# RMSNorm with Silu on one core: 64 KB runs in three buffers and a single SyncE queue, in place of 32 KB runs in six buffers and two queues

## The chip, the cores and the metric

One core of one Trainium2 chip; the other cores idle. The metric is the device time of one execution in microseconds (us). Where two kernels are compared, both ran in the same rounds on the same chip. A quoted ratio is the mean time of one kernel's fast runs over the mean of the other's fast runs of the same rounds, so it isn't quite the ratio of the medians quoted beside it.

In the views, DVE is VectorE, ACT ScalarE, PE TensorE (PEld its weight loads), POOL GpSimd, SP or SPq SyncE, and L88 line 88 of the kernel. A line of a group ends with its count, its busy us and mean ns, and the us that its engine sat idle before it, with what ended the idle time. A line of windows has the stretch in us and its length, then the busy us of PE, PEld, DVE, ACT and POOL.

## The reference

`x` is 8 x 1024 x 2048 fp32, so 8192 rows of 2048, 67.1 MB in and 67.1 MB out.

```python
def reference(x, gamma, eps):
    rms = np.sqrt(np.mean(x ** 2, axis=-1, keepdims=True) + eps)
    out = gamma * x / rms
    return (out * (1 / (1 + np.exp(-out)))).astype(np.float32)
```

## The kernel before

A block is 512 rows, four on each of 128 partitions, 4 MB. ScalarE issues the loads, SyncE the stores: two queues. Six blocks are in flight.

```python
    J = 4
    BUFS = 6
    xb = x2.rearrange("(b p j) d -> b p (j d)", p=P, j=J)      # runs of 4 x 2048 x 4 B = 32 KB
    ...
    def load(b):
        xt = pool.tile([P, J * d], f32, name="xt")
        nc.scalar.dma_start(out=xt, in_=xb[b])                 # queue of ScalarE
    ...
    def multiply(b):                                           # x * rstd * gamma
        for j in range(J):
            nc.vector.scalar_tensor_tensor(out=row(b, j), in0=row(b, j), scalar=rstds[b][:, j:j + 1],
                                           in1=g, op0=ALU.mult, op1=ALU.mult)
    def silu(b):
        for h in range(0, J, 2):                               # two rows at a time
            cols = slice(h * d, (h + 2) * d)
            nc.scalar.activation(out=blocks[b][:, cols], in_=blocks[b][:, cols], func=ACT.Silu)
        store(b)
    def store(b):
        nc.sync.dma_start(out=ob[b], in_=blocks[b])            # queue of SyncE
    ...
```

The squares of a block's rows are shared by ScalarE (Square with an accumulator) and VectorE (a multiply-reduce); the root is ScalarE's, the reciprocal VectorE's. The last block is treated as the change treats all of them: gamma alone on VectorE, rstd as Silu's scale.

Of the kernel before, what the change touches and what calls it, by code (L numbers as in the profile page):

```python
# [1 line left out]

# [4 lines left out]

ACT = mybir.ActivationFunctionType
ALU = mybir.AluOpType


@with_exitstack
def kernel(
    ctx: ExitStack,
    tc: tile.TileContext,
    x: bass.AP,
    gamma: bass.AP,
    eps: bass.AP,
    out: bass.AP,
):  # L20





    nc = tc.nc
    P = nc.NUM_PARTITIONS
    f32 = mybir.dt.float32
    x2 = x.flatten_outer_dims()
    o2 = out.flatten_outer_dims()  # L30
    n, d = x2.shape
    J = 4
    BUFS = 6
    nblk = n // (P * J)
    xb = x2.rearrange("(b p j) d -> b p (j d)", p=P, j=J)
    ob = o2.rearrange("(b p j) d -> b p (j d)", p=P, j=J)

    singles = ctx.enter_context(tc.tile_pool(name="singles", bufs=1))
    pool = ctx.enter_context(tc.tile_pool(name="pool", bufs=BUFS))
    small = ctx.enter_context(tc.tile_pool(name="small", bufs=2))  # L40
    psum = ctx.enter_context(tc.tile_pool(name="psum", bufs=1, space=bass.MemoryType.PSUM))

    Q = 4
    w = d // Q
    grow = singles.tile([P, w], f32)
    g = singles.tile([P, d], f32)
    eps_t = singles.tile([P, 1], f32)
    ones = singles.tile([P, P], f32)
    junk_a = psum.tile([P, d], f32, name="junk_a")
    junk_v = psum.tile([P, d], f32, name="junk_v")  # L50
    blocks, sss, rmss, rstds = {}, {}, {}, {}

    def load(b):
        xt = pool.tile([P, J * d], f32, name="xt")
        nc.scalar.dma_start(out=xt, in_=xb[b])  # L55
        blocks[b] = xt

    def row(b, j):
        return blocks[b][:, j * d:(j + 1) * d]

    def squares_scalar(b, loads=()):


        sss[b] = small.tile([P, J], f32, name="ss")
        for j in range(share(b)):
            nc.scalar.activation(out=junk_a, in_=row(b, j), func=ACT.Square,  # L66
                                 accum_out=sss[b][:, j:j + 1])
            if j == 0:
                for s in loads:
                    load(s)  # L70

    def squares_vector(b):
        for j in range(share(b), J):
            nc.vector.tensor_tensor_reduce(  # L74
                out=junk_v, in0=row(b, j), in1=row(b, j), scale=1.0, scalar=0.0,
                op0=ALU.mult, op1=ALU.add, accum_out=sss[b][:, j:j + 1])

    def share(b):
        return 1 if 4 <= b <= 12 and b % 2 == 0 else 2

    def root(b):
        rms = small.tile([P, J], f32, name="rms")
        nc.scalar.activation(out=rms, in_=sss.pop(b), func=ACT.Sqrt, scale=1.0 / d, bias=eps_t)  # L83
        rmss[b] = rms

    def invert(b):
        rstd = small.tile([P, J], f32, name="rstd")
        nc.vector.reciprocal(out=rstd, in_=rmss.pop(b))  # L88
        rstds[b] = rstd

    def multiply(b):
        for j in range(J):
            nc.vector.scalar_tensor_tensor(out=row(b, j), in0=row(b, j), scalar=rstds[b][:, j:j + 1],  # L93
                                           in1=g, op0=ALU.mult, op1=ALU.mult)

    def silu(b):
        for h in range(0, J, 2):
            cols = slice(h * d, (h + 2) * d)
            nc.scalar.activation(out=blocks[b][:, cols], in_=blocks[b][:, cols], func=ACT.Silu)  # L99
        store(b)  # L100

    def store(b):
        nc.sync.dma_start(out=ob[b], in_=blocks[b])

    with tc.manual_schedule():

        for b in range(BUFS):
            load(b)
        nc.vector.memset(ones, 1.0)  # L109
        nc.vector.memset(eps_t, float(eps))  # L110
        nc.scalar.activation(out=junk_a[:, 0:1], in_=ones[:, 0:1], func=ACT.Square)  # L111
        nc.sync.dma_start(out=grow[0:P:P // Q, :],
                          in_=bass.AP(tensor=gamma.tensor, offset=gamma.offset, ap=[[w, Q], [1, w]]))
        for c in range(Q):
            k = c * (P // Q)
            nc.tensor.matmul(junk_v[:, c * w:(c + 1) * w], ones[k:k + 1, :], grow[k:k + 1, :],  # L116
                             start=True, stop=True)
        nc.vector.tensor_copy(out=g, in_=junk_v)  # L118



        last = nblk - 1
        SOON = 3
        squares_scalar(0)
        squares_vector(0)
        root(0)
        invert(0)
        for b in range(last):
            loads = [b + 3] if BUFS <= b + 3 < nblk else []
            if b < SOON:  # L130
                multiply(b)
                squares_scalar(b + 1, loads)
                silu(b)
                squares_vector(b + 1)
                root(b + 1)
            elif b < last - 1:
                squares_scalar(b + 1, loads)
                squares_vector(b + 1)
                root(b + 1)
                multiply(b)  # L140
                silu(b)
            else:
                multiply(b)
                squares_scalar(b + 1)
                silu(b)
                squares_vector(b + 1)
                root(b + 1)
            if b + 1 < last:
                invert(b + 1)


        for j in range(J):
            if j == J // 2:
                invert(last)
            nc.vector.tensor_mul(out=row(last, j), in0=row(last, j), in1=g)  # L155
        for j in range(J):
            nc.scalar.activation(out=row(last, j), in_=row(last, j), func=ACT.Silu,  # L157
                                 scale=rstds[last][:, j:j + 1])
        store(last)


# [1 line left out]
_INS = ['x', 'gamma', 'eps']  # L163
_OUTS = [((8, 1024, 2048), 'float32')]

_NUMBERS = {'eps': 9.999999747378752e-06}


# [26 lines left out]
```

## Time and profile before

| | before |
|---|---|
| time, median | 316.84 us in the first three runs, 316.9 to 317.0 in all later rounds |
| span of the profiled run | 315.1 us |
| bytes moved | 134.24 MB |
| DMA share of the two data queues | 49.7% + 49.3% |
| VectorE, ScalarE busy | 75%, 68% |

The lines behind this table are in the prediction. One kind of evidence goes below what the page prints: the trace's DMA packet records, each with queue, start, duration and size. They carry no number of the DMA engine. I assigned packets to the 16 engines by joining each packet to the one that ends where it starts (a packet typically starts 3 ns before the last one's end, so sums of gaps can be negative) and has the right size for its place in the queue; every engine then holds the same count, 256 packets before and 152 after. Tables from these records stand in plain fences.

### The profile page before, as it was taken

Reading aid. Unit: us, or ns where it says so; the run is one execution under the profiler, and the core shown is the slowest. Engines: PE = TensorE matmul, PEld = TensorE weight load, DVE = VectorE, ACT = ScalarE, POOL = GpSimd, SP = SyncE. Lnnn points to the kernel's source line nnn. Section 1 sums busy time; section 2 is a strip of 40 time slices with the busy share of each in tenths; the row PEclk is TensorE's granted clock in tenths of the full one; section 3 lists DMA queues with packets and bytes.
Section 4 is the critical chain, followed back from the end, with each engine's and each line's share of the span. In section 5 each row is a group of like instructions: output and inputs, shape, how many; then the busy total and the mean of one; then the engine's idle time right before and its main releaser. Section 6 shows DMA issues by size and latency. Waiting matters only on the chain.

```text
span 315.1 us, 436 instructions
## 1 busy us (share of the span) xinstructions
PE 2.1 (1%) x8; PEld 0.5 (0%) x8; DVE 235.3 (75%) x157; ACT 213.8 (68%) x136; POOL 0.2 (0%) x4
## 2 busy tenths in 40 slices
PE   0200000000000000000000000000000000000000
PEld 0000000000000000000000000000000000000000
DVE  0679597979995695957969489693995939999600
ACT  1349998972799258682687827877288768779910
POOL 0000000000000000000000000000000000000000
DMA  8999999999999999999999999999999999999996
GB/s 334 403 462 403 395 466 399 466 403 462 403 463 403 459 412 453 412 453 420 445 420 445 424 441 424 441 424 441 428 437 437 428 445 420 445 420 445 420 449 287
DMA packets 4618, 134.24 MB, mean 426 GB/s; under 512 B 516, under 2 KB 516, under 8 KB 520
## 3 DMA queue, kind: packets, MB, share of 16 engines
q10 hardware_dynamic: 2304, 67.11, 49.7%
q1 hardware_dynamic: 2312, 67.12, 49.3%
q14 instruction: 2, 0.02, 0.0%
HBM read 67.12 MB, written 67.11 MB: 426 GB/s over the span
## 4 chain that ended last, share of the span: by engine, by line
DMA 68%; DVE 14%; ACT 11%; issue 2%; ACTq 1%; DVEq 0%
DMA xt<-in_x_dram 68%; DVE xt L93 9%; DVE junk_v L74 5%; ACT xt L99 4%; ACT junk_a L66 3%; ACT xt L157 2%; ACT L83 1%; ACTq L190 1%; ACT L157 0%; ACT L99 0%; ACT rms L83 0%; DVE ss L74 0%; DVE rstd L88 0%; ACTq L55 0%; ACTq L83 0%
## 5 line engine op out<-in xcount | busy, mean ns | idle before, releaser
L93 DVE SCALAR_TENSOR_TENSOR xt<-xt,rstd,g 128x2048 f32<-128x2048 f32 x60 | 137.0, 2347 | 0.1
L99 ACT ACTIVATE xt<-xt 128x4096 f32<-128x4096 f32 x30 | 108.3, 3615 | 27.2 <-DVE xt L93 27.1
L74 DVE CUSTOM_DVE_ANT_0 junk_v<-xt 128x2048 f32<-128x2048 f32 x37 | 85.1, 2299 | 42.5 <-DMA xt<-in_x_dram 41.7
L66 ACT ACTIVATE junk_a<-xt 128x2048 f32<-128x2048 f32 x27 | 50.7, 1877 | 22.6 <-DMA xt<-in_x_dram 22.3
L83 ACT ACT_TABLE_LOAD x15 | 19.2, 1283 | 27.6 <-DVE ss L74 27.5
L99 ACT ACT_TABLE_LOAD x14 | 18.0, 1283 | 0.2
L118 DVE COPY g<-junk_v 128x2048 f32<-128x2048 f32 x1 | 2.3, 2292 | 9.4 <-PE junk_v L116 9.4
L88 DVE RECIPROCAL rstd<-rms 128x4 f32<-128x4 f32 x16 | 2.8, 174 | 8.3 <-ACT rms L83 8.3
L155 DVE TENSOR_TENSOR xt<-xt,g 128x2048 f32<-128x2048 f32 x4 | 8.9, 2279 | 0.0
L83 ACT ACTIVATE rms<-ss,eps_t 128x4 f32<-128x4 f32 x16 | 4.8, 297 | 5.7 <-DVE ss L74 5.5
L157 ACT ACTIVATE xt<-xt,rstd 128x2048 f32<-128x2048 f32 x4 | 7.7, 1990 | 0.0
L74 DVE DVE_READ_ACCUMULATOR2_ANT ss<- 128x1 f32 x37 | 5.2, 141 | 0.0
L66 ACT ACTIVATION_READ_ACCUMULATOR junk_a<-xt 128x1 f32 x27 | 5.0, 186 | 0.0
L111 ACT ACT_TABLE_LOAD x1 | 1.3, 1283 | 3.8 <-issue 3.8
L116 PE MATMUL junk_v<-grow,ones 1*128 1x512 f32 x8 | 2.1, 1130 | 8.2 <-DMA grow<-in_gamma_dram 8.2
L157 ACT ACT_TABLE_LOAD x1 | 1.3, 1283 | 0.0
L109 DVE MEMSET ones<- 128x128 f32 x1 | 0.2, 165 | 0.8 <-PEq L176 0.8
L116 PEld LDWEIGHTS junk_v<-grow,ones 1*128 1x128 f32 x8 | 0.5, 307 | 8.2 <-issue 8.2
L111 ACT ACTIVATE junk_a<-ones 128x1 f32<-128x1 f32 x1 | 0.2, 174 | 0.0
L176 POOL MEMSET const-bfloat16-1.0<- 128x1 bf16 x1 | 0.1, 101 | 0.0
L176 POOL MEMSET const-uint8-127<- 128x1 uint8 x1 | 0.1, 101 | 0.0
L176 POOL MEMSET const-float32-0.0<- 128x1 f32 x1 | 0.1, 98 | 0.2 <-issue 0.2
(2 smaller groups left out, 0.2 us busy)
## 6 DMA issues: line engine op xcount, KB each, us to landing
xt<-in_x_dram ACTq DMA_DIRECT2D x16, 4096.0 KB, 38.7
out_dram<-xt SPq DMA_DIRECT2D x16, 4096.0 KB, 29.0
grow<-in_gamma_dram SPq DMA_DIRECT2D x1, 8.0 KB
```

Of the source, the lines that this page charges most:

```text
L66: nc.scalar.activation(out=junk_a, in_=row(b, j), func=ACT.Square, accum_out=sss[b][:, j:j + 1])
L74: nc.vector.tensor_tensor_reduce(out=junk_v, in0=row(b, j), in1=row(b, j), scale=1.0, scalar=0.0, op0=ALU.mult, op1=ALU.add, accum_out=sss ...
L83: nc.scalar.activation(out=rms, in_=sss.pop(b), func=ACT.Sqrt, scale=1.0 / d, bias=eps_t)
L88: nc.vector.reciprocal(out=rstd, in_=rmss.pop(b))
L93: nc.vector.scalar_tensor_tensor(out=row(b, j), in0=row(b, j), scalar=rstds[b][:, j:j + 1], in1=g, op0=ALU.mult, op1=ALU.mult)
L99: nc.scalar.activation(out=blocks[b][:, cols], in_=blocks[b][:, cols], func=ACT.Silu)
L111: nc.scalar.activation(out=junk_a[:, 0:1], in_=ones[:, 0:1], func=ACT.Square)
L116: nc.tensor.matmul(junk_v[:, c * w:(c + 1) * w], ones[k:k + 1, :], grow[k:k + 1, :], start=True, stop=True)
L118: nc.vector.tensor_copy(out=g, in_=junk_v)
L155: nc.vector.tensor_mul(out=row(last, j), in0=row(last, j), in1=g)
L157: nc.scalar.activation(out=row(last, j), in_=row(last, j), func=ACT.Silu, scale=rstds[last][:, j:j + 1])
L190: with _tile.TileContext(nc) as tc:
```

## The change

The intent: longer runs (64 KB a partition), one ordered queue so that loads and stores go in blocks of 8 MB, and a multiply that doesn't wait for rstd.

```diff
-    J = 4
-    BUFS = 6
+    R = 8
+    BUFS = 3
+    loads_of[0] = [4, 4]
+    loads_of[nsup - 1] = stores_of[nsup - 1] = [4, 4]     # halves at the two ends
...
-        nc.scalar.dma_start(out=xt, in_=xb[b])
+            nc.sync.dma_start(out=xt[:, cols(lo, hi)], in_=xs[s][:, cols(lo, hi)])
...
+        for r in range(lo, mid):        # first half of the rows: ScalarE squares
+            nc.scalar.activation(out=junk_a, in_=..., func=ACT.Square, accum_out=...)
+        for r in range(mid, hi):        # second half: VectorE squares
             nc.vector.tensor_tensor_reduce(...)
...
-            nc.vector.scalar_tensor_tensor(out=row(b, j), ..., scalar=rstds[b][:, j:j + 1], in1=g, ...)
+            two = xt[:, cols(r, r + 2)].rearrange("p (r d) -> p r d", r=2)
+            nc.vector.tensor_mul(out=two, in0=two, in1=g.unsqueeze(1).to_broadcast([P, 2, d]))
...
-            nc.scalar.activation(out=blocks[b][:, cols], in_=blocks[b][:, cols], func=ACT.Silu)
+            nc.scalar.activation(out=row, in_=row, func=ACT.Silu, scale=rstd[:, r - lo:r - lo + 1])
+                    nc.sync.dma_start(out=os[s][:, cols(a, b)], in_=xt[:, cols(a, b)])
...
+        for s in range(nsup):
+            for lo, hi in pieces(loads_of[s]):
+                group(s, lo, hi)
+            if s >= 1 and s + 2 < nsup:
+                load(s + 2)
```

The order in the single queue is load 0 (two halves), 1, 2, store 0, 1, load 3, store 2, load 4, store 3, load 5, store 4, load 6, store 5, load 7 (halves), store 6, store 7 (halves): six turns from load to store and five back.

More of the change, by code (lines that the diff above doesn't have):

```diff
@@ L31 @@
     n, d = x2.shape
-    J = 4
-    BUFS = 6
-    nblk = n // (P * J)
-    xb = x2.rearrange("(b p j) d -> b p (j d)", p=P, j=J)
-    ob = o2.rearrange("(b p j) d -> b p (j d)", p=P, j=J)
+    R = 8
+    BUFS = 3
+    nsup = n // (P * R)
+    xs = x2.rearrange("(s p r) d -> s p (r d)", p=P, r=R)
+    os = o2.rearrange("(s p r) d -> s p (r d)", p=P, r=R)
+    loads_of = [[R] for _ in range(nsup)]
+    stores_of = [[R] for _ in range(nsup)]
+    loads_of[0] = [4, 4]
+    loads_of[nsup - 1] = stores_of[nsup - 1] = [4, 4]
     singles = ctx.enter_context(tc.tile_pool(name="singles", bufs=1))
@@ L44 @@
     w = d // Q
-    grow = singles.tile([P, w], f32)
     g = singles.tile([P, d], f32)
@@ L50 @@
     junk_v = psum.tile([P, d], f32, name="junk_v")
-    blocks, sss, rmss, rstds = {}, {}, {}, {}
-    def load(b):
-        xt = pool.tile([P, J * d], f32, name="xt")
-        nc.scalar.dma_start(out=xt, in_=xb[b])
-        blocks[b] = xt
-    def row(b, j):
-        return blocks[b][:, j * d:(j + 1) * d]
-    def squares_scalar(b, loads=()):
-        sss[b] = small.tile([P, J], f32, name="ss")
-        for j in range(share(b)):
-            nc.scalar.activation(out=junk_a, in_=row(b, j), func=ACT.Square,
-                                 accum_out=sss[b][:, j:j + 1])
-            if j == 0:
-                for s in loads:
-                    load(s)
@@ L72, in squares_vector @@
-    def squares_vector(b):
-        for j in range(share(b), J):
-            nc.vector.tensor_tensor_reduce(
-                out=junk_v, in0=row(b, j), in1=row(b, j), scale=1.0, scalar=0.0,
-                op0=ALU.mult, op1=ALU.add, accum_out=sss[b][:, j:j + 1])
-    def share(b):
-        return 1 if 4 <= b <= 12 and b % 2 == 0 else 2
-    def root(b):
-        rms = small.tile([P, J], f32, name="rms")
-        nc.scalar.activation(out=rms, in_=sss.pop(b), func=ACT.Sqrt, scale=1.0 / d, bias=eps_t)
-        rmss[b] = rms
@@ L86, in invert @@
-    def invert(b):
-        rstd = small.tile([P, J], f32, name="rstd")
-        nc.vector.reciprocal(out=rstd, in_=rmss.pop(b))
-        rstds[b] = rstd
-    def multiply(b):
-        for j in range(J):
-            nc.vector.scalar_tensor_tensor(out=row(b, j), in0=row(b, j), scalar=rstds[b][:, j:j + 1],
-                                           in1=g, op0=ALU.mult, op1=ALU.mult)
-    def silu(b):
-        for h in range(0, J, 2):
-            cols = slice(h * d, (h + 2) * d)
-            nc.scalar.activation(out=blocks[b][:, cols], in_=blocks[b][:, cols], func=ACT.Silu)
-        store(b)
@@ L102, in store, with cols, pieces, load @@
-    def store(b):
-        nc.sync.dma_start(out=ob[b], in_=blocks[b])
+    tiles = {}
+    def cols(lo, hi):
+        return slice(lo * d, hi * d)
+    def pieces(sizes):
+        lo = 0
+        for k in sizes:
+            yield lo, lo + k
+            lo += k
+    def load(s):
+        xt = pool.tile([P, R * d], f32, name="xt")
+        for lo, hi in pieces(loads_of[s]):
+            nc.sync.dma_start(out=xt[:, cols(lo, hi)], in_=xs[s][:, cols(lo, hi)])
+        tiles[s] = xt
+    def group(s, lo, hi):
+        xt = tiles[s]
+        k = hi - lo
+        mid = lo + k // 2
+        ss = small.tile([P, R], f32, name="ss")
+        rms = small.tile([P, R], f32, name="rms")
+        rstd = small.tile([P, R], f32, name="rstd")
+        for r in range(lo, mid):
+            nc.scalar.activation(out=junk_a, in_=xt[:, cols(r, r + 1)], func=ACT.Square,
+                                 accum_out=ss[:, r - lo:r - lo + 1])
+        for r in range(mid, hi):
+            nc.vector.tensor_tensor_reduce(
+                out=junk_v, in0=xt[:, cols(r, r + 1)], in1=xt[:, cols(r, r + 1)], scale=1.0, scalar=0.0,
+                op0=ALU.mult, op1=ALU.add, accum_out=ss[:, r - lo:r - lo + 1])
+        nc.scalar.activation(out=rms[:, 0:k], in_=ss[:, 0:k], func=ACT.Sqrt, scale=1.0 / d, bias=eps_t)
+        for r in range(lo, hi, 2):
+            if r == lo + 2:
+                nc.vector.reciprocal(out=rstd[:, 0:k], in_=rms[:, 0:k])
+            two = xt[:, cols(r, r + 2)].rearrange("p (r d) -> p r d", r=2)
+            nc.vector.tensor_mul(out=two, in0=two, in1=g.unsqueeze(1).to_broadcast([P, 2, d]))
+        for r in range(lo, hi):
+            row = xt[:, cols(r, r + 1)]
+            nc.scalar.activation(out=row, in_=row, func=ACT.Silu, scale=rstd[:, r - lo:r - lo + 1])
+            for a, b in pieces(stores_of[s]):
+                if b == r + 1:
+                    nc.sync.dma_start(out=os[s][:, cols(a, b)], in_=xt[:, cols(a, b)])
@@ L105 @@
     with tc.manual_schedule():
-        for b in range(BUFS):
-            load(b)
+        for s in range(BUFS):
+            load(s)
+        nc.scalar.dma_start(out=g[0:P:P // Q, 0:w],
+                            in_=bass.AP(tensor=gamma.tensor, offset=gamma.offset, ap=[[w, Q], [1, w]]))
         nc.vector.memset(ones, 1.0)
@@ L111 @@
         nc.scalar.activation(out=junk_a[:, 0:1], in_=ones[:, 0:1], func=ACT.Square)
-        nc.sync.dma_start(out=grow[0:P:P // Q, :],
-                          in_=bass.AP(tensor=gamma.tensor, offset=gamma.offset, ap=[[w, Q], [1, w]]))
         for c in range(Q):
             k = c * (P // Q)
-            nc.tensor.matmul(junk_v[:, c * w:(c + 1) * w], ones[k:k + 1, :], grow[k:k + 1, :],
+            nc.tensor.matmul(junk_v[:, c * w:(c + 1) * w], ones[k:k + 1, :], g[k:k + 1, 0:w],
                              start=True, stop=True)
         nc.vector.tensor_copy(out=g, in_=junk_v)
-        last = nblk - 1
-        SOON = 3
-        squares_scalar(0)
-        squares_vector(0)
-        root(0)
-        invert(0)
-        for b in range(last):
-            loads = [b + 3] if BUFS <= b + 3 < nblk else []
-            if b < SOON:
-                multiply(b)
-                squares_scalar(b + 1, loads)
-                silu(b)
-                squares_vector(b + 1)
-                root(b + 1)
-            elif b < last - 1:
-                squares_scalar(b + 1, loads)
-                squares_vector(b + 1)
-                root(b + 1)
-                multiply(b)
-                silu(b)
-            else:
-                multiply(b)
-                squares_scalar(b + 1)
-                silu(b)
-                squares_vector(b + 1)
-                root(b + 1)
-            if b + 1 < last:
-                invert(b + 1)
-        for j in range(J):
-            if j == J // 2:
-                invert(last)
-            nc.vector.tensor_mul(out=row(last, j), in0=row(last, j), in1=g)
-        for j in range(J):
-            nc.scalar.activation(out=row(last, j), in_=row(last, j), func=ACT.Silu,
-                                 scale=rstds[last][:, j:j + 1])
-        store(last)
+        for s in range(nsup):
+            for lo, hi in pieces(loads_of[s]):
+                group(s, lo, hi)
+            if s >= 1 and s + 2 < nsup:
+                load(s + 2)
 _INS = ['x', 'gamma', 'eps']
```

## The prediction

> **What bounds the kernel now.** I read the page's totals first, then its slices, then the DMA queues. The totals and the queues:
>
> ```profile
> span 315.1 us, 436 instructions
> PE 2.1 (1%) x8; PEld 0.5 (0%) x8; DVE 235.3 (75%) x157; ACT 213.8 (68%) x136; POOL 0.2 (0%) x4
> ...
> DMA packets 4618, 134.24 MB, mean 426 GB/s; under 512 B 516, under 2 KB 516, under 8 KB 520
> ...
> q10 hardware_dynamic: 2304, 67.11, 49.7%
> q1 hardware_dynamic: 2312, 67.12, 49.3%
> ```
>
> No compute engine is over 75%, while the two queues together hold the 16 DMA engines for 99% of the span (q10 is the loads, issued by ScalarE; q1 the stores, issued by SyncE). Is that 99% real work, or is the rate different when loads and stores share the engines? The windows of the trace answer it: loads alone, the start of sharing, sharing, and the end where the last stores run alone. The last two columns are DMA share and GB/s.
>
> ```profile
> 3.00:40.00 37.00, 2.09 (x8) 0.55 (x8) 24.14 (x17) 24.26 (x20) 0.00 (x0) 1.00 1.00 425
> 40.00:80.00 40.00, 0.00 (x0) 0.00 (x0) 36.42 (x26) 28.26 (x21) 0.00 (x0) 1.00 1.00 433
> 80.00:280.00 200.00, 0.00 (x0) 0.00 (x0) 158.16 (x104) 140.47 (x85) 0.00 (x0) 1.00 1.00 432
> ```
>
> The share is 1.00 in all three. The rate is 432 to 433 GB/s in the shared part and 425 in the first 37 us, where two short disturbances lie (below). The chain that ended last says the same: 68% of it is waiting for loads.
>
> ```profile
> DMA 68%; DVE 14%; ACT 11%; issue 2%; ACTq 1%; DVEq 0%
> ```
>
> Below the page I used the trace's DMA packet records. All 4096 data packets are 32,768 B; the typical one takes 1213 ns, on both queues, whether loads run alone, both alternate, or stores run alone at the end. The four packets of gamma, 2048 B each, take 84 ns. A straight line through the two sizes: (1213 - 84)/(32768 - 2048) = 0.03675 ns per byte, which is 27.2 GB/s an engine and 435 GB/s for 16, plus 84 - 75.3 = 8.7 ns per packet. One engine has 256 packets: 256 x 1.213 = 310.5 us. The first data packet starts 1.7 us into the span, the last ends at 313.9, so 312.2 us hold 310.5 us of packets. The 1.7 us that are missing: the first packet of each engine takes 1.9 us instead of 1.2 (0.7 us), around 36 to 38 us, just after the first store was issued, one packet on each engine takes 1.8 us (0.6 us), and the engines' staggered starts and ends. **The kernel is bound by DMA from end to end, and the engines are full.** The measured time is 1.7 us above the profiled span (316.84 against 315.1).
>
> **What the Trainium skill says.** (1) "DMA: Bandwidth & Descriptors", section "Where 436 GB/s comes from", gives a ceiling of 16 x 32 B x 850 MHz = 435.2 GB/s per core. The slope of my line, 435 GB/s, agrees; the sustained 432 GB/s is 99.3% of it. (2) The same page, "Why small descriptors are slow", puts a fixed cost of some cycles on each packet; the trace shows such a cost, the 8.7 ns of the line above. It is what a longer run can save, and it is small. (3) The same page, "Issuing engines are not separate DMA queues": all DMAs run on the same 16 engines whoever issues them, and several issuers save sequencer time only. The trace agrees as far as it goes: each packet takes 1213 ns with one queue at work or two. (4) "VectorE: DVE Perf Modes", "The perf-mode tier table", has an fp32 tensor_tensor at one element per cycle, 2293 ns for 2048. The trace has 2279 (row L155 below).
>
> **The change, part by part.**
>
> ```profile
> L93 DVE SCALAR_TENSOR_TENSOR xt<-xt,rstd,g 128x2048 f32<-128x2048 f32 x60 | 137.0, 2347 | 0.1
> L99 ACT ACTIVATE xt<-xt 128x4096 f32<-128x4096 f32 x30 | 108.3, 3615 | 27.2 <-DVE xt L93 27.1
> L74 DVE CUSTOM_DVE_ANT_0 junk_v<-xt 128x2048 f32<-128x2048 f32 x37 | 85.1, 2299 | 42.5 <-DMA xt<-in_x_dram 41.7
> L66 ACT ACTIVATE junk_a<-xt 128x2048 f32<-128x2048 f32 x27 | 50.7, 1877 | 22.6 <-DMA xt<-in_x_dram 22.3
> L83 ACT ACT_TABLE_LOAD x15 | 19.2, 1283 | 27.6 <-DVE ss L74 27.5
> L155 DVE TENSOR_TENSOR xt<-xt,g 128x2048 f32<-128x2048 f32 x4 | 8.9, 2279 | 0.0
> L157 ACT ACTIVATE xt<-xt,rstd 128x2048 f32<-128x2048 f32 x4 | 7.7, 1990 | 0.0
> ```
>
> *Runs of 64 KB.* The bytes are unchanged. Per engine, the first and last block's halves stay at 32 KB: 6 transfers of 8 packets, 48 x 1.213 = 58.2 us. The other 208 become 104 packets of 65,536 B, each 0.03675 x 65536 + 8.7 = 2417 ns: 251.4 us. Sum 309.6 against 310.5: **0.9 us saved**, if the hardware takes 64 KB as one packet.
>
> *One queue.* It removes nothing from the engines' work by itself. Loads and stores then alternate in blocks of 8 MB instead of packet by packet. The 0.6 us disturbance at the first store may go with it: 0 to 0.6 us saved.
>
> *VectorE.* 60 multiplies of 2347 ns become pairs of gamma-only multiplies. One of 4096 elements I estimate as 2279 + 2048/0.96 GHz = 4.41 us. Busy: 32 x 4.41 + 32 squares x (2.30 + 0.14 for the read of the accumulator) + about 6 = 225 us, against 235.
>
> *ScalarE.* 30 Silu of 3615 (1.81 us a row) become single rows with a scale at 1.99 (1.92 us apart, from 7.68 us for four in the old last block). Squares rise from 27 to 32; table loads fall from 31 to 21. Busy: 32 x (1.88 + 0.19) + 64 x 1.99 + 21 x 1.28 + 10 x 0.30 = 223 us, against 214. Both engines stay near 71%, so beside the DMA; neither sum goes into the time.
>
> *Does one queue with three buffers keep DMA supplied?* This decides. Order in the queue: load 0 (two halves), load 1, load 2, store 0, store 1, load 3, store 2, load 4, store 3 and so on. A transfer of 8 rows a partition takes 8 x 2.417 = 19.3 us. A block in steady state: its load lands at T, then the queue holds the store before it (issued earlier) and the next load, so the next store must be issued before T + 38.7. Compute from T: four squares on VectorE 9.6 us (ScalarE's four, 8.2, beside them), four double multiplies 17.6, reciprocal 0.2, and two Silu after the last multiply 3.9: T + 31.3. ScalarE alone: 8.2 + 1.3 + 0.3 + 1.3 + 8 x 1.92 = 26.5, shorter. **Slack: 7.4 us**, less about 1.0 us from issue to first packet (0.7 to 1.7 us at the start). The new load waits for the store before last, which landed 10 us earlier. At the start, two halves, load 1 and load 2 keep the engines busy until 61 us, and store 0 is ready at about 45, store 1 at 73 (needed by 80). At the end, the last half lands at about 273; store 6 is ready at 266 and runs to 292, the two last halves are ready at about 281 and 296 and needed at 292 and 302. Nowhere should the engines run dry.
>
> *Sum.* 1.7 (start) + 0.7 (slow first packets) + 309.6 + 0 to 0.6 + 0.3 (stagger) + 1.2 (end, as now) = 313.5 to 314.1 us of span; plus 1.7 gives 315.2 to 315.8.
>
> **Rivals.** *A: the transition inside one queue costs.* If each change from load to store, or back, cost the 0.6 us seen at the first store or the 0.7 of the first load, the 11 changes of this order would add 7 to 8 us: 323, at the edge of slower by 2%. Against it: where both queues work, the engines alternate between loads and stores from packet to packet with no packet longer than 1213 ns to speak of, and at the ends of transfers, with one queue alone (six loads at the start, three stores at the end), no gap appears. But load after store in the same queue is nowhere in this trace. *B: starvation.* If compute took over 38 us per block instead of 31, each period would be extended by the excess, six times; 5 us over would give 30 us, slower by 9%. For it: SyncE issues in order, so a late store also holds back the next load. Against it: the durations above are measured, and only the 4096-wide multiply with a repeated gamma is estimated; it would have to take 6 us instead of 4.4. *C: a run of 64 KB is cut in two anyway.* Then nothing is saved and the time stays at 316 to 317. *D: a real gain of 2%* would need 310.5 us; 134.2 MB at the slope's 435 GB/s are 308.4 us, and start, end and launch of 1.7 + 1.2 + 1.7 make 313. So a gain of more than 1.2% isn't there.
>
> **Range and chances.** The sum's middle is 315.5. I lean a little towards C and small losses at the new transitions: 315.7. Low end: all savings, and smoother starts: 314.7. High end: no saving and a microsecond of new gaps: 317.8. Faster by over 2% contradicts D: 0.01. Slower by over 2% needs A or B: 0.06. Within 2%: 0.93.
>
> **What would show it.** Right: 104 x 16 = 1664 packets of 64 KB at near 2417 ns plus 768 of 32 KB at 1213; DMA share 1.00 in windows from 40 to 280 us; VectorE near 225 and ScalarE near 223 us busy; multiply near 4.41 us; SyncE's stores issued some 6 us before the load ahead of them ends. Wrong: DMA slices below 9 in the middle (A if the queue had work, B if SyncE was then waiting for ScalarE's Silu), or 4096 packets of 32 KB (C). I would be wrong altogether if a 64 KB packet ran at another rate per byte than the line says.

## The result, and the profile after

320.15 us median (319.47 to 320.85, five runs) against 317.0 (316.83 to 317.22): ratio 1.0099, 95% interval 1.0085 to 1.0112. It is 3 us slower, where 315.7 was predicted (1.1 us below the 316.84 that the prediction had), and outside the predicted range of 314.7 to 317.8. "Within 2%" held, because the loss was 1% and not because the sum was right.

The page after: totals, packets, queues.

```profile
span 318.1 us, 386 instructions
PE 2.1 (1%) x8; PEld 0.5 (0%) x8; DVE 216.9 (68%) x109; ACT 218.0 (69%) x160; POOL 0.2 (0%) x4
...
DMA packets 2746, 134.24 MB, mean 422 GB/s; under 512 B 308, under 2 KB 308, under 8 KB 312
...
q1 hardware_dynamic: 2736, 134.22, 98.3%
```

One queue now holds the engines for 98.3%, and neither engine of compute is over 69%. The same windows as in the prediction, with DMA share and GB/s last:

```profile
3.00:40.00 37.00, 2.09 (x8) 0.55 (x8) 26.05 (x15) 22.90 (x21) 0.00 (x0) 1.00 1.02 439
40.00:80.00 40.00, 0.00 (x0) 0.00 (x0) 39.80 (x23) 38.90 (x30) 0.00 (x0) 1.00 1.00 419
80.00:280.00 200.00, 0.00 (x0) 0.00 (x0) 134.16 (x64) 133.78 (x97) 0.00 (x0) 1.00 1.00 433
280.00:300.00 20.00, 0.00 (x0) 0.00 (x0) 16.66 (x8) 17.42 (x14) 0.00 (x0) 1.00 0.97 419
300.00:318.00 18.00, 0.00 (x0) 0.00 (x0) 0.00 (x0) 3.85 (x2) 0.00 (x0) 1.00 0.75 320
```

The middle is full, 433 GB/s against 432. A mean over 16 engines hides what follows; only the last window shows that something runs out late. The groups of the changed compute:

```profile
L88 DVE TENSOR_TENSOR xt<-xt,g 128x4096 f32<-128x4096 f32 x32 | 140.1, 4408 | 7.4 <-ACT junk_a L77 7.4
L91 ACT ACTIVATE xt<-xt,rstd 128x2048 f32<-128x2048 f32 x64 | 124.4, 1994 | 19.9 <-DVE rstd L86 12.2
```

The double multiply takes 4408 ns (4.41 us predicted; (4408 - 2279)/2048 is 1.04 ns for each added element). Its wait for ScalarE's squares (7.4 us in three waits) was not predicted: the first multiply overwrites rows that ScalarE is still squaring. When SyncE issued its DMAs (start, stretch covered, line, count; L65 is a load, L94 a store):

```profile
100.64 0.33 SPq L94 DMA_DIRECT2D out_dram<-xt  x1
...
151.41 0.33 SPq L94 DMA_DIRECT2D out_dram<-xt  x1
...
191.40 0.33 SPq L94 DMA_DIRECT2D out_dram<-xt  x1
...
231.36 0.33 SPq L94 DMA_DIRECT2D out_dram<-xt  x1
...
270.45 33.75 SPq L94 DMA_DIRECT2D out_dram<-xt  x3
```

These are stores 2 to 5 and the last three. By the packet records their turns came at 119.9, 158.8, 197.6, 236.3 and 275.0 (median engine), so each was in the queue 4.5 us or more ahead: SyncE didn't starve the queue. Only the very last half store was late; SyncE issued it at 303.9, the median engine had run dry at about 304.0 and began it at 304.8.

Where the 2.9 us of span are, from the packet records of the engine that ends last (us). A typical packet takes the commonest time of its size; the excess is what an engine's packets took above that:

```
                       start   packets if all were typical   excess over typical   gaps    end     span
before, last engine     1.93   256 x 1.213 = 310.53              1.81             -0.34   313.93  315.13
after,  last engine     1.76   48 x 1.213 + 104 x 2.418 = 309.70 5.23             -0.06   316.64  318.05
before, median engine   1.95   310.53                            1.53             -0.80   313.21
after,  median engine   1.95   309.70                            2.40              0.47   314.52
```

The saving is there (0.8 us). The excess over typical packets eats it: 0.9 us more on the median engine, 3.4 us more on the last. And the last engine is now 2.1 us behind the median, where it was 0.7 behind. Which packets are long? Nearly all are the last load packet ahead of a store. (L7b is the second half of load 7; lag is how much later an engine gets somewhere than the median one.)

```
after: excess of the last packet of each transfer, ns (mean over the engines / largest)
ahead of a turn load -> store:  L2 1094/1390   L3 155/456   L4 344/921   L5 213/1138   L6 124/476   L7b 14/151
ahead of a turn store -> load:  S1 8/124       S2 5/78      S3 0/0       S4 0/0        S5 0/0
after: lag of the latest engine behind the median, us, at the start of each transfer
S0 0.31 | S1 0.31 L3 0.40 S2 0.38 | L4 0.79 S3 1.42 | L5 1.42 S4 2.56 | L6 2.56 S5 3.01 | L7 3.01 S6 3.01 S7a 3.01 S7b 2.20
before: the same every 24 packets from packet 96 to the end: 0.73 0.73 0.72 0.72 0.72 0.72 0.72, end 0.72
```

Before, one engine was pushed back at 109 us by a 309 ns packet of the instruction queue, with a data packet 353 ns too long just after it, and stayed 0.72 us behind to the end. After, an engine was pushed back in the same way at 132 us (lag from 0.35 to 0.79), and then its lag grew at the next three turns from load to store, and only there: 0.79, 1.42, 2.56, 3.01. The last turn added nothing. The drop to 2.20 at the end is the other engines waiting for the late last store.

Theory T1, from this: **in one queue all engines turn from loading to storing at about the same time; an engine that lags still loads while the others store, and there its load packets are slowed, so that it loses about as much again as it lags.** In two queues every engine alternates packet by packet, and there is no common turn. Rivals: T2, the late last store sets the end; T3, the 64 KB packets themselves do harm; and the compute part.

### The profile page after: what moved, and what is told of

Same layout as the page of the kernel before. It is cut to its first block, busy times and chain, and to the rows that moved or that the text cites. A ratio compares the mean times of both kernels' runs of the same rounds, so it can differ in the third digit from the quotient of the medians.

```text
span 318.1 us, 386 instructions
## 1 busy us (share of the span) xinstructions
PE 2.1 (1%) x8; PEld 0.5 (0%) x8; DVE 216.9 (68%) x109; ACT 218.0 (69%) x160; POOL 0.2 (0%) x4
## 3 DMA queue, kind: packets, MB, share of 16 engines
q1 hardware_dynamic: 2736, 134.22, 98.3%
## 4 chain that ended last, share of the span: by engine, by line
DMA 42%; DVE 36%; ACT 9%; another core or an unknown queue 4%; issue 4%; ACTq 1%; SPq 0%; DVEq 0%
DMA xt<-in_x_dram 31%; DVE xt L88 27%; DMA out_dram<-xt 11%; DVE junk_v L80 8%; ACT xt L91 7%; ACT junk_a L77 2%; ACTq L145 1%; DVE ss L80 0%; DVE rstd L86 0%; SPq L94 0%; DVEq L145 0%; DVEq L80 0%
## 5 line engine op out<-in xcount | busy, mean ns | idle before, releaser
L88 DVE TENSOR_TENSOR xt<-xt,g 128x4096 f32<-128x4096 f32 x32 | 140.1, 4408 | 7.4 <-ACT junk_a L77 7.4
L91 ACT ACTIVATE xt<-xt,rstd 128x2048 f32<-128x2048 f32 x64 | 124.4, 1994 | 19.9 <-DVE rstd L86 12.2
L80 DVE CUSTOM_DVE_ANT_0 junk_v<-xt 128x2048 f32<-128x2048 f32 x32 | 73.6, 2299 | 65.7 <-DMA xt<-in_x_dram 64.9
L77 ACT ACTIVATE junk_a<-xt 128x2048 f32<-128x2048 f32 x32 | 60.1, 1878 | 56.8 <-DMA xt<-in_x_dram 56.1
L77 ACT ACTIVATION_READ_ACCUMULATOR junk_a<-xt 128x1 f32 x32 | 6.0, 186 | 0.0
L80 DVE DVE_READ_ACCUMULATOR2_ANT ss<- 128x1 f32 x32 | 4.5, 141 | 0.0
L83 ACT ACTIVATE rms<-ss,eps_t 128x8 f32<-128x8 f32 (+1 forms) x10 | 3.0, 300 | 0.1
L106 PE MATMUL junk_v<-g,ones 1*128 1x512 f32 x8 | 2.1, 1131 | 8.0 <-DMA g<-in_gamma_dram 8.0
L86 DVE RECIPROCAL rstd<-rms 128x8 f32<-128x8 f32 (+1 forms) x10 | 1.9, 185 | 0.0
```

Source lines behind the costliest of these rows:

```text
L77: nc.scalar.activation(out=junk_a, in_=xt[:, cols(r, r + 1)], func=ACT.Square, accum_out=ss[:, r - lo:r - lo + 1])
L80: nc.vector.tensor_tensor_reduce(out=junk_v, in0=xt[:, cols(r, r + 1)], in1=xt[:, cols(r, r + 1)], scale=1.0, scalar=0.0, op0=ALU.mult, op ...
L83: nc.scalar.activation(out=rms[:, 0:k], in_=ss[:, 0:k], func=ACT.Sqrt, scale=1.0 / d, bias=eps_t)
L86: nc.vector.reciprocal(out=rstd[:, 0:k], in_=rms[:, 0:k])
L88: nc.vector.tensor_mul(out=two, in0=two, in1=g.unsqueeze(1).to_broadcast([P, 2, d]))
L91: nc.scalar.activation(out=row, in_=row, func=ACT.Silu, scale=rstd[:, r - lo:r - lo + 1])
```

## The experiments

### Two queues again, all else as changed

```diff
-                    nc.sync.dma_start(out=os[s][:, cols(a, b)], in_=xt[:, cols(a, b)])
+                    nc.scalar.dma_start(out=os[s][:, cols(a, b)], in_=xt[:, cols(a, b)])
```

> The changed kernel with its stores issued by ScalarE, so that loads and stores are again in two queues; 64 KB runs, three buffers and compute as they are. Theory T1 (in one queue the last load packet ahead of a store is slowed, unevenly over the 16 engines, and the slowest engine sets the end): the long load packets ahead of stores go, except once at the first store (about 0.6 to 1.1 us per engine), sum of packet time per engine near 310.5 to 311.5 us instead of 312.4, and the time falls from 320.2 to about 316 to 317.5. Theory T2 (the end is set by the last store, which is issued late because the multiply waits for ScalarE's squares): the tail remains or gets worse, time 319 to 322. Theory T3 (64 KB packets themselves are the harm): 319.5 to 320.5.

Measured: 320.39 us (319.51 to 320.83), ratio 1.0106 (1.0092 to 1.012). A miss for T1's number, and inside the ranges of T2 and T3. The rates over the 40 slices of its page tell where:

```profile
GB/s 330 440 416 527 395 395 395 395 510 411 395 437 477 395 411 502 403 404 485 411 411 403 485 420 411 395 502 411 403 485 407 399 428 424 444 416 444 416 337 276
```

The loss is in the last two slices: 13 of 16 engines stand idle for 1.3 to 3.1 us at 307 us, ahead of the last half store, which ScalarE issued at 305.9. The last half load had landed only at 286 us, which is where VectorE begins on it; in the one-queue kernel the last load packets end by 278. The two ends of the delay:

```profile
286.13 2.30 DVE L80 CUSTOM_DVE_ANT_0 junk_v<-xt 128x2048 f32<-128x2048 f32 x1 [1.40 <-DMA xt<-in_x_dram]
305.93 0.34 ACTq L94 DMA_DIRECT2D out_dram<-xt  x1
```

The other three engines had no such idle and still ended last, at 317.1 to 317.2. **They show that lags grew here too, in two queues:** their packets took 5.8 to 6.0 us above typical, those of the median engine 2.7. They also made the landing late. When the other engines turned to store 6 at 275 us, these three, 2.8 us behind, still had three load packets to go; one was slowed by 0.7 us, and the last two then took turns with store packets, so the load's last packets ended at 283.3 (and its completion came one store packet later, at 285.7) instead of near 275. So with three large buffers, two queues don't bring the time back. T1 had said that the long packets would go, the first store's excepted. They did not: growing lags need no single queue.

### 32 KB runs in the one queue

```diff
-        for lo, hi in pieces(loads_of[s]):
+        for lo, hi in pieces([4, 4]):                      # loads: always two transfers of 4 rows
             nc.sync.dma_start(out=xt[:, cols(lo, hi)], in_=xs[s][:, cols(lo, hi)])
...
-                    nc.sync.dma_start(out=os[s][:, cols(a, b)], in_=xt[:, cols(a, b)])
+                    for lo4 in range(a, b, 4):             # stores likewise
+                        nc.sync.dma_start(out=os[s][:, cols(lo4, lo4 + 4)], in_=xt[:, cols(lo4, lo4 + 4)])
```

> The changed kernel, one queue, same groups and order, but each transfer of 8 rows issued as two of 4 rows, so all runs are 32 KB. T1 with a cost in proportion to the packet: the long packet at the first turn from load to store falls from 1.1 to about 0.55 us, the later ones from 0.1-0.35 to half; against that 0.9 us more for twice the packets: time 318.5 to 320. T1 with a fixed cost per turn: 320.5 to 321.5. T3: close to the kernel before, 316.8 to 317.5.

Measured: 319.35 us (318.77 to 319.57), ratio 1.0075 (1.0062 to 1.0088). It is some 0.8 us under the changed kernel in spite of twice as many packets, and 2.5 us over the kernel before. So T3 explains at most a part. The time lies in T1's range for a cost in proportion to the packet, but not for that reason. The first turn costs as much as with 64 KB, 1.10 us a mean engine, now spread over two packets; it isn't in proportion to the packet. Later turns, from the packet records (lag of the engine when its last load packet ahead of the store begins, excess of its last two packets):

```
turn       latest engine: lag us, excess ns     second: lag, excess      median engine: excess
L4 -> S3       0.79        297                   0.59    162                 6
L5 -> S4       1.30        785                   0.74    594                 8
L6 -> S5       2.55        767                   1.93    703                68
```

An engine in step loses nearly nothing, one that lags loses hundreds of nanoseconds. At the last turn (L7 -> S6) the two latest, 2.61 and 2.17 us behind, lost less: 126 and 278 ns.

### The tail: no wait of the multiply for ScalarE's squares

```diff
-        for r in range(lo, mid):
+        for r in range(mid, hi):
             nc.scalar.activation(out=junk_a, ...Square...)
-        for r in range(mid, hi):
+        for r in range(lo, mid):
             nc.vector.tensor_tensor_reduce(...)
```

> The changed kernel with the halves of the squares exchanged: VectorE squares the first half of the rows, ScalarE the second, so the first multiply no longer waits for ScalarE's squares of the rows that it overwrites. The last store should be issued 5 to 6 us earlier and the idle of about 0.3 to 1.3 us ahead of it, seen on 14 of 16 engines, should go. T2: the time falls by 0.8 to 1.5 us, to 318.7 to 319.4. T1: the slowest engine had no such idle, so the time falls by 0 to 0.3 us, within the scatter of 319.5 to 320.9.

Measured: 319.96 us (319.28 to 320.43), ratio 1.0095 (1.0081 to 1.0108); no difference to 1.0099 that the intervals allow. The wait went, and the last two half stores now read (SyncE's issues; the stretch ends with the second):

```profile
286.06 14.86 SPq L94 DMA_DIRECT2D out_dram<-xt  x2
```

The last one was issued 3 us earlier, at 300.6 instead of 303.9. The idle ahead of it is gone on all engines, and the median engine ends at 313.58 instead of 314.52. But the latest engine ends at 316.92 (316.64 before the edit): its lag ran 1.01, 1.99, 2.88, 2.96, 3.34 us at the starts of stores 2, 3, 4, 5, 6. **T2 falls:** removing the tail's wait moves 14 engines and not the end.

### One queue alone, in the kernel before

```diff
-        nc.scalar.dma_start(out=xt, in_=xb[b])
+        nc.sync.dma_start(out=xt, in_=xb[b])
...
-        nc.sync.dma_start(out=grow[0:P:P // Q, :],
+        nc.scalar.dma_start(out=grow[0:P:P // Q, :],
```

> The kernel before with its loads moved to SyncE's queue beside the stores (gamma to ScalarE's, so that it does not wait behind six loads); 32 KB runs, six buffers, 4 MB transfers, compute as before. T1: about 11 turns from load to store in this order; with 0.6 us at the first and 0.1 to 0.2 on average at the others, and a slowest engine that loses more, the time rises from 317.0 to 318.5 to 320.5. If one queue costs nothing: 316.5 to 317.2.

Measured: 321.17 us (320.22 to 321.4), ratio 1.0129 (1.0115 to 1.0143), above T1's range. This is the plainest result: 32 KB runs, six buffers and the old compute, and the one queue alone costs 4.3 us, more than the whole change. The page has almost the same busy times as the kernel before, and a lower last slice:

```profile
span 319.6 us, 446 instructions
...
PE 2.1 (1%) x8; PEld 0.5 (0%) x8; DVE 235.3 (74%) x157; ACT 213.6 (67%) x136; POOL 0.2 (0%) x4
...
GB/s 325 439 418 455 402 451 439 385 422 455 402 455 427 428 444 410 447 431 422 451 402 459 418 422 455 406 451 422 431 443 414 447 426 418 451 410 451 431 422 111
```

The packet records: at the ten turns from load to store after the first, the median engine loses 0 ns every time. Engines behind by 0.5 to 4.3 us lose 200 to 800 ns at many turns. The median engine ends at 313.3 (313.2 before), so the queue didn't run dry; the last ends at 318.4. Its lag was 0.84 us at the first store, 2.82 at store 5, 4.75 at store 11 and 5.1 at the end. Some turns cost a lagging engine nothing (at one, engines 2.2 and 1.97 us behind lost 0 and 6 ns), so "as much again as it lags" is a tendency and no law.

### The compute part alone

The kernel before with double multiplies by gamma and Silu by rows with rstd as scale (the same lines as in the change's diff; two queues, 32 KB, six buffers).

> The kernel before with only the compute part of the change: gamma-only multiplies of two rows, Silu row by row with rstd as its scale; two queues, 32 KB runs, six buffers as before. All theories but one: compute is beside a full DMA, so 316.5 to 317.3. If the slower ScalarE path (about 9 us more busy time) reached the DMA, 318 or more.

Measured: 317.15 us (317.02 to 317.76), ratio 1.0008 (0.9995 to 1.0022). Busy times moved as they do in the change, and the time didn't:

```profile
span 315.6 us, 445 instructions
...
PE 2.1 (1%) x8; PEld 0.5 (0%) x8; DVE 229.2 (73%) x127; ACT 221.8 (70%) x166; POOL 0.2 (0%) x4
```

### More turns

Starting from the 32 KB one-queue kernel: the two stores of 4 rows and the two loads of 4 rows alternate.

```diff
+                for lo, hi in pieces([4, 4]):
+                    store_piece(s, lo, hi)
+                    if s >= 1 and s + 2 < nsup:
+                        load_piece(s + 2, lo, hi)
```

> As the one-queue kernel with 32 KB runs, but each store of 4 rows is followed by a load of 4 rows, so the direction turns about twice as often (12 turns from load to store instead of 7); packets, bytes and compute are the same. T1 in its sharper form (an engine that lags behind the others finds them storing while it still loads, and loses about as much again as it lags, at each turn, up to some 3 us): more turns let a lag grow further, 320.5 to 322 against 319.35. If the cost were per packet or per transfer: 319 to 319.7.

Measured: 320.26 us (320.08 to 320.57), ratio 1.0104 (1.009 to 1.0118), against 1.0075 (1.0062 to 1.0088) with fewer turns. (The turns from load to store are 11 here against 6; the text on record counts 12 and 7, and the next one seven as well.) It is 0.9 us slower for the same packets and bytes, a little under the range T1 gave, and clearly above the one without it. The last engine ends at 317.35 instead of 316.31.

### A nudge to one engine, in one queue and in two

```diff
+        spare = nc.dram_tensor("spare", (1, 8191), f32, kind="Internal").ap()
+        nc.scalar.dma_start(out=spare, in_=bass.AP(tensor=x.tensor, offset=x.offset, ap=[[8191, 1], [1, 8191]]))
```

In the kernel before the same two lines, issued by SyncE. The length was chosen so that the copy stays in one packet on one engine; the trace shows it as one packet of 32,764 B and 1213 ns, at 8.5 us in the one-queue kernel and 9.0 in the other.

> The changed kernel with one extra packet of 32 KB (some 1.2 us) on a single DMA engine at the start, copied between two places of HBM and not used. T1 in its sharper form: that engine's lag grows at each of the seven turns, so the time rises by more than the nudge if no other engine would have lagged as far anyway: 321 to 323.5. If lags do not grow: at most 1.2 us more, and only if that engine would have ended late: 320.2 to 321.3.

> The kernel before (two queues) with the same extra packet on a single engine at the start. T1: loads and stores alternate on every engine, there are no common turns, the lag stays what it is, and the time rises by 0.5 to 1.2 us, to 317.4 to 318.1. If two queues also made lags grow: 319 or more.

Measured: one queue 320.14 us (319.9 to 320.41), ratio 1.01 (1.0086 to 1.0113), which is no change against 320.15. Two queues 317.47 us (317.39 to 317.93), ratio 1.0017 (1.0004 to 1.003), half a microsecond more. The time of the first missed what T1 expected. The lag of the nudged engine says what happened:

```
one queue:  lag us at the start of  L0b 1.11  L2 1.11 | S0 1.80  L3 1.78 | S2 2.72  L4 2.67 | S3 2.67 | S4 3.05 | S5 3.26 | S6 3.62
two queues: lag us every 24 packets from packet 24:     1.52 1.49 1.49 1.46 1.46 1.46 1.45 1.45 1.45 1.45, end 1.45
```

In one queue the same nudge that keeps its size in two grows to 3.6 us, at turns from load to store. But its growth is uneven: one turn (L4 -> S3) added nothing to a lag of 2.67 us. Without the nudge another engine reaches 3.0 to 3.3 by itself; so the end, which goes by the worst engine, hardly moves (316.9 against 316.6). That a nudged engine's lag grows is as T1 says; its step "a nudge makes the time longer" was wrong. It is no ceiling near 3 us that stopped the lag: with one queue in the kernel before, an engine ended 5.1 us behind. Why the growth slows is not shown.

### Stores that wait until the load ahead has landed

```diff
                 if b == r + 1:
+                    ahead = 2 if s == 0 else s + 1
+                    if s != 1 and ahead < nsup:          # 512 B out of the tile that is being loaded
+                        nc.sync.dma_start(out=spare[s:s + 1, :], in_=tiles[ahead][0:1, R * d - 128:R * d])
                     nc.sync.dma_start(out=os[s][:, cols(a, b)], in_=xt[:, cols(a, b)])
```

> The changed kernel, one queue, but ahead of each store that follows a load in the queue a 512 B copy out of the end of that load's tile, which SyncE can issue only when the load has landed: no engine stores while another still loads. T1 in its sharper form: the last load packets ahead of stores take 2418 ns again on all engines (under 0.1 us over it, the first turn perhaps excepted), no engine's lag grows over 1.2 us; but each of the seven turns now has an idle gap of 1.5 to 3 us, so the time rises to 329 to 340. If the turn itself, not the neighbours, slowed the last load packet: the long packets stay beside the gaps, and lags grow as before.

Measured: 331.64 us (331.64 to 331.81), ratio 1.0466 (1.0452 to 1.0479), within what was expected of T1. There are six such waits (the text on record says seven). One microsecond at one of them, DMA share and GB/s last:

```profile
121.50:122.50 1.00, 0.00 (x0) 0.00 (x0) 0.35 (x1) 0.35 (x1) 0.00 (x0) 1.00 0.00 0
```

The idle ahead of the six stores is 1.83 to 2.00 us on average over the engines, 11.5 us in all, as much as lies between 331.64 and 320.15. With no engine storing while another loads, the last load packet ahead of a turn is typical again: excess 0 to 2 ns on average, 23 at most, where it was 14 to 1094 on average and 1390 at most; even the first turn's 1.1 us is gone. No engine was more than 0.50 us behind after the start. So the long load packets need stores that are under way, or queued, before the load has ended. The wait takes away the other engines' stores and the engine's own queued one alike; against its own speaks that with one queue in the kernel before, the median engine lost 0 ns at ten turns with its own store right behind the load.

It left a riddle. The last store packets ahead of a load, which cost nothing in the changed kernel, now exceed the typical by 0.6 to 0.8 us on average at five turns. There all engines began the store within 0.1 us of each other. So the waits moved the cost more than they removed it: the median engine's packets took 5.3 us above typical, against 2.4 in the changed kernel. I have no tested explanation.

### Two tries at a faster version

One: 64 KB runs, stores in ScalarE's queue, squares exchanged, the last block loaded as one transfer, its last stores 4, 2 and 2 rows.

> A try at a version better than both: 64 KB runs with stores in ScalarE's queue, squares exchanged, last block loaded in one transfer and its last half stored in two of 2 rows. If only the tail and the 32 KB against 64 KB sharing of the last block cost the two-queue version its gain: 315.8 to 317. If three buffers leave stretches in which only loads or only stores run, with turns in common and lags: 318 to 320.

Measured: 322.51 us (322.27 to 322.72), ratio 1.0176 (1.0163 to 1.0189). A miss. The engines idle twice at the end, 1.9 to 3.9 us ahead of the packets of the last block's first half store at 298 and 1.4 to 1.7 us more at 309: loaded as one transfer, the last block can't be started until all of it has landed.

Two: the same with 32 KB runs everywhere and stores as soon as 4 rows are done.

> The same idea with 32 KB runs: two queues, every transfer of 4 rows, stores issued as soon as 4 rows are done, three tiles of 8 rows, squares exchanged. With finer transfers loads and stores should overlap more evenly: 316.5 to 318. If lags grow here too: 318.5 to 320.

Measured: 322.15 us median, but at two levels: 318.26 and 318.84 in two runs, 321.92 to 322.77 in four; ratio 1.0124 (1.0079 to 1.0168). The upper level is above both ranges expected. The profiled run was at that level; most of its engines idle 1.1 to 3.8 us ahead of the last 4-row store, at 308 us, and two engines that didn't idle ended last. The packets of these two took 6.9 and 7.7 us above typical, against 2.5 on the median engine: lags grew in two queues again. What sets the level is open. Neither try beats the kernel before.

## Why the prediction was wrong

- **The bound** was read rightly: DMA from end to end. Compute is beside it (compute alone: ratio 1.0008). The sums of busy time were too high, 225 and 223 us where the page has 216.9 (VectorE) and 218.0 (ScalarE): the union that the page prints counts overlapping records once, the sums twice.
- **64 KB as one packet** was right: 1664 packets of 65,536 B at 2418 ns (2417 predicted), and the typical packets sum to 0.8 us less per engine (0.9 predicted).
- **Supply** was right in the middle: stores were in the queue 4.5 us or more ahead of their turns (about 6 predicted). At the end it was wrong by 8 us: the last half store was ready at 303.9, not 296. Some 3.3 us of that are the multiply's wait for ScalarE's squares, which the schedule left out (without it, 300.6). Most of the rest was there one block earlier: compute on block 6 began at 239.6, where the schedule has about 234 (273 less 38.7), for a block waits for the engine that is furthest behind (the median one had its part at 236.3, the last at 239.3). The late store idled the median engine some 0.8 us, and undoing the wait left the time where it was.
- **The failed step is the sum's "0.3 (stagger)", together with "0 to 0.6" for the disturbance at the first store.** The sum treated 16 engines as one. In place of 0.3, the last engine ended 2.1 us behind the median one, and would have been 3.0 behind had the others not waited for the last store. In place of 0 to 0.6, the first turn cost 1.1 us, and later ones 0.1 to 0.3 on a mean engine. On the last engine the excess was 5.23 us where the sum allowed for 0.7 to 1.3.
- **Rival A** named the right place, a change of direction inside one queue, and was argued away by evidence from two queues, where the alternation hides it. It was also too simple: it charged each change to every engine alike. What the runs show, after the first turn, is a cost that an engine in step hardly pays (0 ns at ten turns with 32 KB, up to 0.3 us with 64 KB) and a lagging one pays at most turns. One queue alone, in the kernel before, costs 1.3% (321.17).
- **Rivals B and C** didn't happen; the gain was bounded as D said.

Shown: the one queue is a sufficient cause, in the kernel before; the late engine sets the end; lags grow at turns from load to store in one queue, and stay constant in two with six buffers; the long load packets vanish if no store is issued before the load has landed. Shown too: the one queue is not necessary, since with three buffers lags grew in two queues as well. So which part of the change hurts, the queue or the three large buffers, has no single answer: lags grew with either alone. Argued only: that it is the other engines' stores that slow a lagging engine's load. Open: why lags grow at some turns and not at others, the first store's 0.7 to 1.3 us on all engines, and the two levels of the last try.

## What to carry to other kernels

If DMA is the bound, count the latest of the 16 DMA engines, not their mean: a share of 1.00 in the windows can hide one engine that is 3 us behind. Mixing loads and stores packet by packet, from two queues with six buffers, kept every lag at its first size; gathering them into blocks in one queue let lags grow, and so did two queues with three large buffers. And look for evidence on a change of structure in a part of the trace that already has that structure; if there is none, the range must be wider than the arithmetic of the rest suggests.

## What the Trainium skill lacked or had wrong

- "DMA: Bandwidth & Descriptors", "Issuing engines are not separate DMA queues", says that several issuers save sequencer time only. Here moving the loads into the stores' queue, with nothing else changed but gamma's small load, cost 1.3% (316.9 to 321.2 us): the queues also decide how loads and stores mix on each engine.
- No page has the growth of an engine's lag at a common turn from load to store: 0.79, 1.42, 2.56, 3.01 us in one queue, 0.72 throughout in two with six buffers.
- The same page, "Why small descriptors are slow", stops at small sizes. Here a run of 64 KB was one packet of 2418 ns, 8 ns less than two of 32 KB at 1213: 0.8 us per engine in 134 MB, less than what the turns cost.
- No page has the cost of the first store beside loads: 0.7 to 0.9 us on each engine in two queues with 32 KB runs and 1.1 to 1.3 with 64 KB, 1.1 in one queue, and none if the load has landed.
